# Mixer stage of a transformer block: convs, conv norm and conv half of the output product placed earlier, query-norm factors made in two halves

## The chip, the core and the metric

The kernel runs on one core of a Trainium2 chip. The metric is the device time of one execution in microseconds (us). The engines are PE (TensorE: matrix products, with PEld for the loads of its stationary operand), DVE (VectorE), ACT (ScalarE), POOL (GpSimd) and SP (SyncE, which issues the transfers). Each engine works through its own queue in the order in which the program was laid down and waits for others by semaphores.

## The reference, cut to what matters

The kernel computes two transformer layers' worth of blocks on a sequence of 512 positions with 1024 channels. The change lies in the first stage, the mixer (S = 512, 8 query heads of 64, 2 key heads; weights in fp32):

```python
def parallel_mixer(h, w_in, conv_dw, ..., w_out, tabs):
    z = jnp.einsum("bsd,dc->bsc", h, w_in)
    a_val, a_gate = z[..., :CONV_CH], z[..., CONV_CH:o0]
    q, k, v = ...
    a = a_val * jax.nn.sigmoid(a_gate)
    a = dwconv_centred(a, conv_dw, conv_dw_b)      # 31 taps, 512 channels
    a = layernorm(a, conv_ln_g, conv_ln_b)
    a = jax.nn.silu(a)
    q = apply_axial_rope(rmsnorm(q, q_norm_g), tabs)
    k = apply_axial_rope(rmsnorm(k, k_norm_g), tabs)
    att = gqa_blocked(q, k, v)
    mixed = jnp.concatenate([a, att], axis=-1)
    return jnp.einsum("bsc,cd->bsd", mixed, w_out)
```

Behind the mixer come a cross attention to a memory of 256 positions, five feed-forward stages, a pooling mixer and a latent attention. The keys and values of the memory do not depend on the mixer, and the kernel computes them inside it, as work that fills PE's waits.

## The kernel before

Activations lie as channels by positions, in tiles of 128 x 512. A product in fp32 precision is made of three passes (`mm3`, lines 182 to 184): weights and activations are each split into a rounded half `hi` and the rest `lo`. For weights `fetch` (L143) has SP load a tile of 128 x 1024 into one of three raw buffers; `cook` has ACT round it (`whi`, L152) and DVE subtract (`wlo`, L154), which frees the raw buffer.

The mixer, in the order of the program:

- *Projections.* `linear` over 14 column tiles of `w_in`, 24 products (8 x 3) each, in the order of `ORDER`: gate and value tiles in turn (`ev_gate`, `ev_val`, whose product `at` is a conv's input), the key tile, the value tile, four query tiles (`ev_q`). `ev_q` takes the sums of squares of the queries into one PSUM tile `qsum`; when all four are in, `inner_rstd` makes the factor `fcol` of all eight heads: a transpose on PE, then three Newton steps on DVE (L246 to L249).
- *Heads.* For each of 8 heads `scores` makes four score tiles (L707, L708), and `softmax_rows` their exponentials: maximum on DVE (L451), its product with the factor (`nb`, L452), exponential on ACT (L454), reciprocal on DVE (L455), scaling on POOL (L456). `attend` transposes the four results in blocks (L138 `pt`, four per block), ACT and DVE split each block (`pth`, `ptl`), and two products per block add up `po` (L723, L724). ACT copies half of it (`low`), DVE adds (`mixf`, L730). Two heads make one tile of `mix`. `scores(n + 1)` stands ahead of `attend(n)`.
- *Convs.* `conv` makes one of four 128-channel tiles: its weights take a raw buffer; 16 copies through SP (L587) bring the input at several shifts into the one set of tiles `cx`, so the copies of a conv wait for PE's end of the conv before. 24 products of 32 columns by 512 (L593, four of them side by side in PE), an evacuation by ACT, 7 taps by DVE (L602). They stand in the program at heads 0, 0, 1 and 2 (`CONV_AT`).
- *Conv norm.* `conv_norm` is a generator in three steps (mean, variance, the normalised and gated tiles `cv`), one step at each of heads 4, 5 and 6 (`CN_AT`).
- *Memory keys and values.* The generator `mem_kv` makes eight key tiles (24 products of 256 columns each) and 96 value products of 512 columns; two steps stand at each head (`KV_HEAD`).
- *Output product.* 8 column blocks in 8 PSUM tiles at once (all the PSUM there is), first the half of the attention (`mix`, 96 products), then that of the conv (`cv`, 96), then the evacuations.

What stands where in the queues is not the program's order alone: the tile framework lays the instructions down by their priority in the program and by when it thinks buffers and operands are there. So a step can stand ahead of others that the program names first, and buffers go to whoever the framework thinks can have them first.

```python
tags = ["ps", "ps", "po", "mi", "sc", "sc", "pt", "pt"]
pss = [self.ps(t, "wo") for t in tags]
for half, xh in ((0, mix), (1, cv)):
```

## Time and profile before

| | |
|---|---|
| median of 3 runs | 2541.47 us (2541.29 to 2543.51) |
| the profiled execution | 2543.81 us, its span 2542.0 us |
| busy: PE, DVE, ACT, POOL | 2491.3, 1305.2, 916.3, 301.8 us |
| granted clock of PE, mean | 0.996 |
| mixer, up to the warm-up products behind its output product | 302.69 us |

Times in the rows are from the span's start. A row of the view in order of time has the start, the duration, the engine, the line, the operation, output <- inputs, shapes and a count; in square brackets the time that the engine was idle before and what ended it. The ends of products are modelled, so that one can seem to overlap the next. Each key, value or weight tile has the name of its buffer (`raw`, `whi`, `wlo`); `ps` are products in PSUM, `sc` scores, `wo` the output product. The granted clock (PEclk) is a share of 2.4 GHz.

### The profile page before, as it was taken

The page shows a single profiled execution, that of the slowest core. Times are in us where ns is not written, and L with a number is a line of the kernel's source. Part 1 is how long each engine was busy: PE and PEld are TensorE (multiplying, and loading weights), DVE is VectorE, ACT ScalarE, POOL GpSimd, SP SyncE. Part 2 cuts the span into 40 slices and gives each one's busy share as a digit, 9 for nine tenths or more (in the row PEclk, how much of TensorE's full clock was granted, in tenths as well). Part 3 has the DMA queues.
Part 4 walks back from the last instruction along what each step waited for, and adds up shares of the span by engine and source line. Part 5 has one row for each costly group of instructions (what it writes and reads, how often), then busy time and mean ns, then how long its engine had stood idle before and what let it go on. Part 6 is the DMA issues. An engine that isn't in the chain of part 4 may idle for free.

```text
span 2542.0 us, 29816 instructions
## 1 busy us (share of the span) xinstructions
PE 2491.3 (98%) x11900; PEld 2015.1 (79%) x11900; DVE 1305.2 (51%) x1906; ACT 916.3 (36%) x1324; POOL 301.8 (12%) x285
## 2 busy tenths in 40 slices
PE   8898999999999999999999999999999999999999
PEld 6656677888887888888888888888887777888887
DVE  5777453766624554435555533554334685555522
ACT  4445444544423332224333222332223454423321
POOL 0011112111100111002111100111000012111100
PEclk9999999999999999999999999999999999999999
DMA  5143222232332223333223333232332211232332
GB/s 191 61 125 97 67 67 67 83 99 92 95 100 79 95 96 100 93 99 115 91 93 98 100 97 98 93 98 97 94 99 92 75 59 33 93 100 92 97 108 77
DMA packets 71851, 235.52 MB, mean 93 GB/s; under 512 B 8544, under 2 KB 12256, under 8 KB 71712
## 3 DMA queue, kind: packets, MB, share of 16 engines
q1 hardware_dynamic: 70336, 231.08, 29.1%
q0 software_dynamic: 1232, 2.36, 0.4%
q8 instruction: 93, 1.52, 0.2%
q14 instruction: 46, 0.38, 0.0%
q10 hardware_dynamic: 144, 0.18, 0.0%
HBM read 227.33 MB, written 2.10 MB: 90 GB/s over the span
## 4 chain that ended last, share of the span: by engine, by line
PE 94%; DVE 4%; ACT 1%; issue 1%; DMA 0%; ACTq 0%; DVEq 0%
PE ps L183 28%; PE ps L182 28%; PE ps L184 28%; PE cps L593 1%; PE pt L138 1%; PE sum L222 1%; PE bc L290 1%; PE wo L183 1%; PE wo L184 1%; PE wo L182 0%; PE po L724 0%; ACT whi L152 0%; DVE wlo L154 0%; PE po L183 0%; PE sc L182 0%
## 5 line engine op out<-in xcount | busy, mean ns | idle before, releaser
L152 ACT CAST whi<-raw 128x1024 fp32r<-128x1024 f32 (+2 forms) x432 | 440.2, 1021 | 1214.9 <-PE ps L183 754.1
L154 DVE TENSOR_TENSOR wlo<-raw,whi 128x1024 fp32r<-128x1024 f32 (+2 forms) x428 | 591.3, 1384 | 509.1 <-ACT whi L152 503.9
L182 PE MATMUL ps<-xh,whi 128*128 128x512 f32 x2008 | 782.7, 391 | 7.9 <-ACT xh L203 7.1
L183 PE MATMUL ps<-xl,whi 128*128 128x512 f32 x2008 | 785.5, 391 | 3.2 <-DVE xl L384 2.5
L184 PE MATMUL ps<-xh,wlo 128*128 128x512 f32 x2008 | 782.3, 390 | 0.0
L182 PEld LDWEIGHTS ps<-xh,whi 128*128 128x128 f32 x2008 | 377.7, 188 | 88.8 <-ACT xh L203 7.1
L183 PEld LDWEIGHTS ps<-xl,whi 128*128 128x128 f32 x2008 | 377.7, 188 | 87.3 <-DVE xl L384 6.1
L184 PEld LDWEIGHTS ps<-xh,wlo 128*128 128x128 f32 x2008 | 377.7, 188 | 78.1 <-issue 0.6
L182 PE MATMUL ps<-ah,whi 128*128 128x512 f32 x880 | 342.3, 389 | 0.0
L183 PE MATMUL ps<-al,whi 128*128 128x512 f32 x880 | 342.3, 389 | 0.0
L184 PE MATMUL ps<-ah,wlo 128*128 128x512 f32 x880 | 342.3, 389 | 0.0
L902 DVE TENSOR_TENSOR g<-ps,bct 128x512 f32<-128x512 f32 x176 | 120.7, 691 | 392.5 <-PE ps L184 384.2
L907 POOL TENSOR_TENSOR g<-g 128x512 f32<-128x512 f32 x88 | 118.9, 1351 | 887.3 <-ACT whi L152 624.4
L182 PEld LDWEIGHTS ps<-ah,whi 128*128 128x128 f32 x880 | 165.2, 188 | 34.3
L184 PEld LDWEIGHTS ps<-ah,wlo 128*128 128x128 f32 x880 | 165.2, 188 | 34.3
L183 PEld LDWEIGHTS ps<-al,whi 128*128 128x128 f32 x880 | 165.2, 188 | 34.2
L333 POOL TENSOR_TENSOR sq<-sq 128x512 f32<-128x512 f32 x54 | 81.5, 1510 | 582.0 <-ACT sq L326 581.4
L199 ACT CAST ah<-g 128x512 fp32r<-128x512 f32 x88 | 54.7, 622 | 113.3 <-POOL g L907 113.3
L456 POOL TENSOR_SCALAR p<-p,rl 128x512 f32<-128x512 f32 (+3 forms) x80 | 51.6, 650 | 334.5 <-DVE rl L455 277.0
L441 DVE SCALAR_TENSOR_TENSOR x<-ps,x 128x512 f32<-128x512 f32 x40 | 27.5, 691 | 84.5 <-PE ps L184 84.3
L201 DVE TENSOR_TENSOR al<-g,ah 128x512 fp32r<-128x512 f32 x88 | 63.1, 717 | 8.1 <-ACT ah L199 7.7
L454 ACT ACTIVATE p<-sc,nb,f 128x512 f32<-128x512 f32 (+3 forms) x80 | 53.5, 674 | 34.0 <-DVE nb L452 33.9
(293 smaller groups left out, 2314.5 us busy)
## 6 DMA issues: line engine op xcount, KB each, us to landing
raw<-in_wgu SPq DMA_DIRECT2D x176, 512.0 KB, 3.5
raw<-in_wd SPq DMA_DIRECT2D x64, 512.0 KB, 3.5
raw<-in_w_up SPq DMA_DIRECT2D x44, 512.0 KB, 3.5
raw<-in_wd SPq DMA_DIRECT2D x32, 384.0 KB, 3.1
raw<-in_w_down SPq DMA_DIRECT2D x16, 512.0 KB, 3.6
raw<-in_w_in SPq DMA_DIRECT2D x14, 512.0 KB, 3.7
raw<-in_mla_w_in SPq DMA_DIRECT2D x9, 512.0 KB, 3.5
raw<-in_mla_w_q SPq DMA_DIRECT2D x12, 384.0 KB, 3.0
```

The costliest lines, as they stand in the source:

```text
L152: self.nc.scalar.copy(hi[:, s], raw[:, s])
L154: eng.tensor_tensor(out=lo[:, s], in0=raw[:, s], in1=hi[:, s].bitcast(F32), op=ALU.subtract)
L182: mm(ps, w[0], x[0], start=start, stop=False)
L183: mm(ps, w[0], x[1], start=False, stop=False)
L184: self.mmi = mm(ps, w[1], x[0], start=False, stop=stop)
L199: nc.scalar.copy(hi, src)
L201: self.loi = eng.tensor_tensor(out=lo, in0=src, in1=hi.bitcast(F32), op=ALU.subtract)
L333: self.nc.gpsimd.tensor_tensor(out=sqs[0][:, :w], in0=sqs[0][:, :w], in1=sq[:, :w], op=ALU.add)
L454: nc.scalar.activation(p[:, :w], ps[:, :w], AF.Exp, bias=nb, scale=f, accum_out=l)
L456: nc.gpsimd.tensor_scalar(out=p[:, :w], in0=p[:, :w], scalar1=rl, scalar2=1.0, op0=ALU.mult, op1=ALU.mult)
L902: nc.vector.tensor_tensor(out=g, in0=ps, in1=rb, op=ALU.mult)
L907: nc.gpsimd.tensor_tensor(out=g, in0=g, in1=st["g"], op=ALU.mult)
```

## The change

Two convs go into the projections (behind the 7th and the 10th tile), two to head 0; the steps of the conv norm to heads 2, 3 and 4. The output product begins with the conv half: its column blocks 0 to 5 are made one by one in the `ps` tiles of PSUM and copied to SBUF by ACT (`part`), blocks 6 and 7 stay in PSUM; then comes the half of the attention, for blocks 0 to 5 into PSUM tiles that the heads have left, and DVE adds the parts. The factor of the query norms is made in two halves of four heads.

```diff
-    CONV_AT = (0, 0, 1, 2)
-    CN_AT = (4, 5, 6)
+    CONV_IN, CONV_AT = (6, 9), (0, 0)
+    CN_AT = (2, 3, 4)
...
-            i = nt - 10
+            i, o = (nt - 10) % 2, P * ((nt - 10) // 2)
             sq = self.square(ps)
-            self.sums([(self.c("blk64")[:, 32 * i:32 * i + 32], sq)], ps=qsum, start=i == 0,
-                      stop=i == 3)
+            self.sums([(self.c("blk64")[:, 32 * i:32 * i + 32], sq)], ps=qsum, o=o,
+                      start=i == 0, stop=i == 1)
+            if i == 1:
+                fcol.append(self.inner_rstd(qsum[:, o:o + P], 64, R1, 4, post=64.0 ** -0.5))
...
-        fcol = self.inner_rstd(qsum[:, :P], 64, R1, 8, post=64.0 ** -0.5)
+            if n in self.CONV_IN:
+                accs.append(self.conv(len(accs), ats[len(accs)]))
...
-                c = 8 * j + 2 * i + h
-                prs[n].append(self.softmax_rows(sc, S, fcol[:, c:c + 1], "xs"))
+                c = 4 * j + 2 * (i % 2) + h
+                prs[n].append(self.softmax_rows(sc, S, fcol[i // 2][:, c:c + 1], "xs"))
...
+        unit = lambda half, u: self.tiles(self.load_unit(a["w_out"][half, u]), 8)
+        parts = []
+        for u in range(4):
+            ws = unit(1, u)
...
+            for n2 in range(2):
+                ps = self.ps("ps", "wo")
+                for k in range(4):
+                    self.mm3(ps, ws[4 * n2 + k], cv[k], k == 0, u < 3 and k == 3)
+                if u < 3:
+                    nc.scalar.copy(room[n2], ps)
+                    parts.append(room[n2])
+                else:
+                    parts.append(ps)
         evac = self.post_collect("g_mixpost")
-        for nt in range(8):
-            evac(nt, pss[nt])
+        tags = ["sc", "sc", "po", "mi", "pt", "pt"]
+        for u in range(4):
+            ws = unit(0, u)
+            for n2 in range(2):
+                nt = 2 * u + n2
+                ps = parts[nt] if u == 3 else self.ps(tags[nt], "wo")
+                for k in range(4):
+                    self.mm3(ps, ws[4 * n2 + k], mix[k], u < 3 and k == 0, k == 3)
+                if u < 3:
+                    nc.vector.tensor_tensor(out=parts[nt], in0=ps, in1=parts[nt], op=ALU.add)
+                evac(nt, parts[nt])
```

Three places show how this moves instructions. The first is SP's queue where the loads of the memory's keys begin, before (`raw` with a number is one load into one of the three raw buffers, `in_conv_d` a conv's weights, `cx` a copy of a conv's input; in brackets the semaphores that the entry waits for):

```order
L143 DMA raw_1186<-in_conv_d 128x768 [waits DMAHW4_49,DMAHW2_49,DVE_49]
L487 DMA mem_769<-in_memT 128x2x256 [waits DMAHW7_49,DVE_49]
L143 DMA raw_1241<-in_w_mem_k 128x1024 [waits DMAHW5_49,DVE_49]
L143 DMA raw_1273<-in_w_mem_k 128x1024 [waits DMAHW4_49,DVE_49]
L143 DMA raw_1409<-in_conv_d 128x768 [waits DMAHW6_49,DMAHW5_49,DVE_49]
L587 DMA cx_254<-at_490 32x504 [waits PE_49]
```

and with the change:

```order
L588 DMA cx_257<-at_709 32x503 [waits DMAHW4_49]
L143 DMA raw_1315<-in_conv_d 128x768 [waits DMAHW5_49]
L143 DMA raw_1370<-in_w_mem_k 128x1024 [waits DMAHW6_49,DVE_49]
L143 DMA raw_1402<-in_w_mem_k 128x1024 [waits DMAHW7_49,DMAHW6_49,DVE_49]
L143 DMA raw_1543<-in_w_mem_k 128x1024 [waits DMAHW7_49,DMAHW0_49,DVE_49]
L143 DMA raw_1575<-in_w_mem_k 128x1024 [waits DMAHW1_49,DMAHW0_49,DVE_49]
L143 DMA raw_1713<-in_w_mem_k 128x1024 [waits DMAHW2_49,DMAHW1_49,DVE_49]
L143 DMA raw_1745<-in_w_mem_k 128x1024 [waits DMAHW3_49,DMAHW2_49,DVE_49]
L143 DMA raw_1895<-in_w_mem_k 128x1024 [waits DMAHW4_49,DMAHW3_49,DVE_49]
L143 DMA raw_1927<-in_w_mem_k 128x1024 [waits DMAHW5_49,DMAHW4_49,DVE_49]
L143 DMA raw_2112<-in_w_mem_v 128x1024 [waits DMAHW5_49,DVE_49]
L588 DMA cx_254<-at_910 32x504 [waits PE_49]
```

Before, two key tiles were loaded ahead of the second conv's copies and the others between later convs. Now all eight and the first value unit stand in a row, behind the 16 copies of the third conv, and each waits for the load before it and for DVE: they pass one raw buffer, while the other two hold the weights of the third and fourth conv.

The second place is DVE's queue at the factor of the query norms (`y_`, `b_`: Newton steps; `f_`: the factor; `nb_`: a score tile's maximum times it), before:

```order
L246 SCALAR_TENSOR_TENSOR b_967<-y_966,v_961 128x32
L248 TENSOR_TENSOR b_967<-b_967,y_966 128x32
L249 SCALAR_TENSOR_TENSOR y_966<-b_967,y_966 128x32
L277 SCALAR_TENSOR_TENSOR f_962<-y_966,y_238 128x32
L452 TENSOR_SCALAR nb_985<-mx_984,f_962 128x1
```

and with the change:

```order
L249 SCALAR_TENSOR_TENSOR y_960<-b_961,y_960 128x16
L533 TENSOR_TENSOR mk_1540<-ps_1549,mbc_115 128x256
L154 TENSOR_TENSOR wlo_1578<-raw_1575,whi_1577 128x1024
L246 SCALAR_TENSOR_TENSOR b_961<-y_960,v_955 128x16
L248 TENSOR_TENSOR b_961<-b_961,y_960 128x16
L249 SCALAR_TENSOR_TENSOR y_960<-b_961,y_960 128x16
L277 SCALAR_TENSOR_TENSOR f_956<-y_960,y_238 128x16
```

The `lo` half of the fourth key tile (`raw_1575` above) stands between the second and the last Newton step of the first half's factor now.

The third is PE's queue at the end of the last head (`po`; `mixh` is the half of the attention, `ch` that of the conv), before:

```order
L138 MATMUL pt_2480<-con_113,p_2317 128x128
L724 MATMUL po_2446<-ptl_2475,vh_589 128x512
L723 MATMUL po_2446<-pth_2485,vh_589 128x512
L724 MATMUL po_2446<-ptl_2486,vh_589 128x512
L182 MATMUL wo_2545<-mixh_1405,whi_2582 128x512
L183 MATMUL wo_2545<-mixl_1406,whi_2582 128x512
```

and with the change:

```order
L729 MATMUL po_2471<-pth_2499,vh_589 128x512
L182 MATMUL wo_2692<-ch_2180,whi_2675 128x512
L183 MATMUL wo_2692<-cl_2181,whi_2675 128x512
L184 MATMUL wo_2692<-ch_2180,wlo_2676 128x512
L730 MATMUL po_2471<-ptl_2500,vh_589 128x512
L729 MATMUL po_2471<-pth_2510,vh_589 128x512
L182 MATMUL wo_2729<-mixh_1534,whi_2707 128x512
L730 MATMUL po_2471<-ptl_2511,vh_589 128x512
```

Before, 147 products of the output stood behind the last product of the last head, and 92 of them and 4 more were the whole conv half. Now the conv half is through ahead of it, and 86 products of the other half are left. Behind the mixer only some neighbouring instructions change places, in later stages.

## Rows read from the trace of the kernel before

**Rows 1.** The page: the span.

```profile
span 2542.0 us, 29816 instructions
```

**Rows 2.** Two stretches of the mixer; columns as in the first line.

```profile
core 0: us, PE busy (x) PEld busy (x) DVE busy (x) ACT busy (x) POOL busy (x), PEclk, DMA share, GB/s
112.00:118.00 6.00, 5.44 (x16) 3.60 (x16) 3.87 (x11) 3.04 (x8) 2.78 (x4) 0.57 0.00 0
247.00:254.00 7.00, 3.58 (x11) 2.71 (x12) 3.93 (x8) 4.37 (x7) 0.00 (x0) 0.50 0.00 0
```

**Rows 3.** PE in order of time: start, duration, what; score products of head 0.

```profile
112.06 0.80 PE L707 MATMUL sc<-kh,st 128*128 128x512 f32 x1 [5.78 <-ACT p L454]
112.65 0.63 PE L708 MATMUL sc<-kl,st 128*128 128x512 f32 x1
113.08 0.63 PE L707 MATMUL sc<-kh,st 128*128 128x512 f32 x1
```

**Rows 4.** PE: a product of a key tile and the one 24 later.

```profile
103.01 0.28 PE L184 MATMUL ps<-mh,wlo 128*128 128x256 f32 x1
...
105.89 0.28 PE L184 MATMUL ps<-mh,wlo 128*128 128x256 f32 x1
```

**Rows 5.** PE: end of the tenth w_in tile.

```profile
74.12 0.39 PE L184 MATMUL ps<-xh,wlo 128*128 128x512 f32 x1
```

**Rows 6.** PE: 21 conv products in a row, two records each.

```profile
142.18 5.34 PE L593 MATMUL cps<-cx,raw 128*32 128x512 f32 x42
```

**Rows 7.** PE: four transposes of a head, and what starts after them.

```profile
148.02 0.60 PE L138 MATMUL pt<-con,p 128*128 128x128 f32 x4
148.38 0.36 PE L182 MATMUL ps<-mh,whi 128*128 128x256 f32 x1
```

**Rows 8.** SP: issues of two key tiles, and of the 16 copies of one conv tile.

```profile
82.69 6.35 SPq L143 DMA_DIRECT2D raw<-in_w_mem_k  x2
...
165.56 10.02 SPq L587 DMA_DIRECT2D cx<-at  x16
```

**Rows 9.** The DMA view: one of the copies, last number us to landing.

```profile
cx<-at SPq DMA_DIRECT2D x16, 64.0 KB, 2.0
```

**Rows 10.** ACT rounds two key tiles that share a raw buffer.

```profile
143.56 1.05 ACT L152 CAST whi<-raw 128x1024 fp32r<-128x1024 f32 x1
...
150.37 1.05 ACT L152 CAST whi<-raw 128x1024 fp32r<-128x1024 f32 x1 [4.63 <-DMA raw<-in_w_mem_k]
```

**Rows 11.** DVE ends heads 1, 5 and 7.

```profile
158.36 0.68 DVE L730 TENSOR_TENSOR mixf<-po,low 64x512 f32<-64x512 f32 x1
...
237.34 0.69 DVE L730 TENSOR_TENSOR mixf<-po,low 64x512 f32<-64x512 f32 x1 [2.98 <-ACT low L727]
...
268.49 0.68 DVE L730 TENSOR_TENSOR mixf<-po,low 64x512 f32<-64x512 f32 x1 [1.20 <-ACT low L727]
```

**Rows 12.** Groups by line and shape, 98 to 303 us: busy us, mean ns.

```profile
L154 DVE TENSOR_TENSOR wlo<-raw,whi 128x1024 fp32r<-128x1024 f32 x24 | 29.4, 1239 | 31.1 <-ACT whi L152 31.1
...
L454 ACT ACTIVATE p<-sc,nb,f 128x512 f32<-128x512 f32 x32 | 24.8, 777 | 24.8 <-DVE nb L452 24.8
L451 DVE TENSOR_REDUCE mx<-sc 128x1 f32<-128x512 f32 x32 | 21.7, 681 | 9.1 <-PE sc L708 9.0
L201 DVE TENSOR_TENSOR ptl<-pt,pth 128x512 fp32r<-128x512 f32 x32 | 21.6, 680 | 3.9 <-ACT pth L199 3.7
...
L199 ACT CAST pth<-pt 128x512 fp32r<-128x512 f32 x32 | 18.5, 586 | 8.5 <-PE pt L138 8.4
...
L452 DVE TENSOR_SCALAR nb<-mx,f 128x1 f32<-128x1 f32 x32 | 6.1, 204 | 0.2
...
L602 DVE SCALAR_TENSOR_TENSOR acc<-at,cwh,acc 128x504 f32<-128x504 f32 x8 | 5.9, 733 | 0.0
```

**Rows 13.** PE: after the last head, and the end of the product.

```profile
269.23 0.50 PE L182 MATMUL wo<-mixh,whi 128*128 128x512 f32 x1 [1.39 <-DVE mixf L730]
...
302.69 1.04 PE L435 MATMUL warm<-idb 128*128 128x512 bf16 x4
```

More of the change, by code (lines that the diff above doesn't have):

```diff
@@ L664, in ev_v @@
                 vh.append(hl)
-        qs = []
+        qs, fcol = [], []
         qsum = self.ps("po", "qsum")
         def ev_q(nt, ps):
-            i = nt - 10
+            i, o = (nt - 10) % 2, P * ((nt - 10) // 2)
             sq = self.square(ps)
-            self.sums([(self.c("blk64")[:, 32 * i:32 * i + 32], sq)], ps=qsum, start=i == 0,
-                      stop=i == 3)
+            self.sums([(self.c("blk64")[:, 32 * i:32 * i + 32], sq)], ps=qsum, o=o,
+                      start=i == 0, stop=i == 1)
+            if i == 1:
+                fcol.append(self.inner_rstd(qsum[:, o:o + P], 64, R1, 4, post=64.0 ** -0.5))
             qr = self.rope(ps, "gq", "gqs", cos, sin)
@@ L739, in mixer @@
             attend(n)
-            for i in range(4):
-                if n == self.CONV_AT[i]:
-                    accs.append(self.conv(i, ats[i]))
+            for _ in range(self.CONV_AT.count(n)):
+                accs.append(self.conv(len(accs), ats[len(accs)]))
             for _ in range(self.KV_HEAD):
@@ L747, in mixer @@
         self.wshare = self.W_OUT
-        tags = ["ps", "ps", "po", "mi", "sc", "sc", "pt", "pt"]
-        pss = [self.ps(t, "wo") for t in tags]
-        for half, xh in ((0, mix), (1, cv)):
-            for u in range(4):
-                ws = self.tiles(self.load_unit(a["w_out"][half, u]), 8)
-                for n2 in range(2):
-                    for k in range(4):
-                        self.mm3(pss[2 * u + n2], ws[4 * n2 + k], xh[k], half == 0 and k == 0,
-                                 half == 1 and k == 3)
-        evac = self.post_collect("g_mixpost")
-        for nt in range(8):
-            evac(nt, pss[nt])
+        unit = lambda half, u: self.tiles(self.load_unit(a["w_out"][half, u]), 8)
+        parts = []
+        for u in range(4):
+            ws = unit(1, u)
+            if u < 2:
+                room = self.big("part")
+                room = [room[:, :S], room[:, S:2 * S]]
+            elif u == 2:
+                room = [self.t("pr", name="part") for _ in range(2)]
+            for n2 in range(2):
[7 more added lines that the diff above has]
+                    parts.append(ps)
+        evac = self.post_collect("g_mixpost")
+        tags = ["sc", "sc", "po", "mi", "pt", "pt"]
[9 more added lines that the diff above has]
+                evac(nt, parts[nt])
     def conv_norm(self, accs, cv):
```

## The prediction

> **What bounds the kernel now.** I read the clock and busy table by stretches first, then PE in order of time in the mixer, then what ended its waits, then the queues of SP and DVE at those places. Behind the mixer PE works almost without a gap, and the change leaves the order of work there as it was, so only the first 303 us can move. The span is 2542.0 us [rows 1]; that execution took 2543.8 us as a whole, 2.3 above the median of 2541.47. I work out a difference on the span and take it off the median.
>
> In the mixer PE stands in two places. After the projections the first score products of head 0 are done, and the next one waits 5.78 us for an exponential, which waits for the factor of the query norms [rows 3]. Near the end PE holds the sums of the conv norm in its queue ahead of the last heads; there, from 247 to 254 us, it is busy 3.58 of 7 us at a granted clock of 0.50, and behind the first place at 0.57, that is near the lower of its two levels, 1.2 GHz [rows 2]. Heads 1 to 7 end at 158.36 to 268.49 us [rows 11]; PE takes up the out product at 269.23 and has done it by 302.69 [rows 13]. By the order, 147 products of 512 columns lie between, so one takes 0.228 us (33.46 / 147).
>
> **The change, part by part.** *Two convs move into the projections.* Their loads of weights there run tiles ahead of PE, so I price the move on PE alone: 21 conv products in a row take 5.34 us [rows 6], 24 take 6.1, two convs 12.2. That is work moved, not added. The tenth tile of w_in, which ends at 74.4 (74.12 and one product) [rows 5], and the second conv behind it end at 86.6.
>
> *SP's queue.* The 16 copies of the third conv wait for that second conv and take SP 10.0 us. All eight key tiles of the memory stand behind them, so the first is issued at 96.6 instead of 82.69 [rows 8]. Two of the three raw buffers now hold conv weights until those convs have run. Key tiles go through the third, one after the other. One such turn (rounding by ACT, the lo half by DVE, the next load) takes 6.81 us from one rounding to the next [rows 10]. I take this for each, so the seventh key tile is ready 7 x 6.81 = 47.7 us later, at 144.3.
>
> *Query factors in two halves.* These add one transpose and some 15 DVE instructions of about 0.2 us, as the small ones that scale a maximum [rows 12], 3 us. What they should hide, the 5.78 us, is hidden by key products now. But DVE has the lo half of the fourth key tile ahead of the last Newton steps, so the early factor comes no earlier than that tile. I cost the halves at nothing: the key chain covers them. Without that cover they would cost their 3 us.
>
> *The chain through the third and fourth conv.* PE's queue has seven key tiles ahead of the third conv: the seventh takes 2.88 [rows 4], the conv 6.1, to 153.3. The fourth conv's copies take 10.0 and 2.0 to land [rows 8, 9], to 165.3; its last 21 products stand behind the last of them, 5.3, to 170.6. ACT's evacuation is nearest to a 0.59 us cast [rows 12], to 171.2. Then DVE has, up to the end of head 1, 7 taps, 4 maxima, 7 small ones, 2 lo halves of 512 columns, 4 of 1024 and the head's own sum: 5.1 + 2.7 + 1.4 + 1.4 + 5.0 + 0.7 = 16.3 [rows 12]. Head 1 ends at 187.5, 28 us later than before, but with all the convs, all the keys and half the values done.
>
> *Heads 2 to 7.* For each I add up what the three queues hold between the ends of two heads, with the durations of [rows 12] and 0.228 per product and 0.09 per transpose [rows 7]; the largest of the three is the head's least time. Head 2 on DVE: 4 maxima, 5 splits, 7 small, 1 sum, 8.1. In this way DVE sets heads 2 to 4 with 8.1, 16.6 and 18.8, ACT head 5 with 11.1, PE heads 6 and 7 with 13.4 and 14.0 (46 and 48 out products among them): 82.0. The same count for heads 2 to 5 of the kernel before gives 18.2 + 22.6 + 15.1 + 19.8 = 75.7, and they took 79.0 (158.36 to 237.34), 1.043 times as much. So 82.0 x 1.043 = 85.5, and the last head ends at 273.0, 4.5 us later than before. The six copies and six adds of the partial products are in these counts or beside the last products, 3.5 and 4.1 us in all.
>
> *The end.* 0.74 us later (as from 268.49 to 269.23) PE goes on. All 96 products of the conv half are ahead of the last head now, so 86 remain: 19.6 us, to 293.3. Before it was 302.69. The work of the evacuation behind the last product is the same, since the last two column blocks stay in PSUM. **Sum: 9.4 us less**, 2541.5 - 9.4 = 2532.
>
> On the clock, the rows show a fall behind a wait of 5.78 us [rows 2, 3]. In the key chain PE will have some 3 us of wait in each turn (6.8 less 2.9 and about 1 of head work), shorter than that one; my sum takes the upper level there. The Trainium skill (TensorE: Matmul & The Clock Gate, the section HAM oscillation — how this bites in real kernels) says that short bursts of products between waits for loads can start at the lower clock again each time. By that rule the sum would be that of the second rival; the trace agrees for the 5.78 us wait and leaves shorter ones open.
>
> **The rivals.** *All overlaps* (chance 0.17). For it: two issues of key tiles together once took 6.35 us, and an issue is up to 0.63 of that (10.02 / 16 for a copy) [rows 8], so one turn was 5.7 to 6.35, in the middle 6.0, and nothing forces the factor 1.043. Then 7 x 0.8 = 5.6 and 3.5 more are saved: 18.5 less, 2523.
> *The lower clock in the key chain* (0.18). A 512-column product takes 0.43 us there [rows 3] for 0.228. The seventh key tile and the third conv, on the chain, double: 9.0 later, 2541, no change. For it: the waits in each turn; against it: the head's work between.
> *The key chain is slower than its load* (0.15). A lo half that waits on DVE behind work that itself waits for PE lengthens every turn, as the one for the sixth key tile does, behind two maxima of head 1. The gain is gone at a turn of 8.2 us (6.8 + 9.4 / 7). At 9.5, a turn and four such instructions, it is 18.8 later: 9.4 slower, 2551. For it: in 31.1 us DVE waited for a rounding before a lo half [rows 12]. Against it: before, the maxima were between them as well, and the turn was 6.81.
> That the change does not do what it says can only hold for the early factor, above, and is in the sum.
>
> **How the numbers follow.** My own case has 0.50, 2526 to 2538 by a turn 0.8 us shorter or longer. About 5 us (0.2%) is what a measurement of this kernel tells from no change. Of my case nearly all lies below 2536.4, the first rival lies there whole: faster 0.65. The second, and the upper edge of mine: same 0.20. The third: slower 0.15. The range leaves out the third and a little of the first: 2519 to 2546.
>
> **What would show it.** Right: PE's wait of 5.78 us is gone, replaced by several of about 3 us that end on lo halves of key tiles; roundings of key tiles 6 to 7 us apart; head 1 ends near 187, head 7 near 273, the warm-up products begin near 293; no stretch at 0.50 near the conv norm. Wrong: turns above 8 us; waits of PE for loads of w_in in the projections, which I cost at nothing (their loads lead by two tiles, and a stall there would come on top whole); a last head that ends after 283.

## The result: slower by 0.5%, and the profile after

The changed kernel takes 2554.59 us (median of 5 runs, 2553.44 to 2556.74) where the kernel before takes 2543.51 beside it: a ratio on record of 1.0051, with a 95% interval of 1.0040 to 1.0063 (these two medians alone give 1.0044; in the larger batches beside the experiments the kernel before has medians of 2541.91 to 2542.78). The forecast was 2532.0, with a range of 2519 to 2546. One execution of one experiment below took 8835.65 us; it is left out (the other one of that run took 2543.32), and the run was repeated.

The profiled execution has this span (from the page; before: [rows 1]):

```profile
span 2552.8 us, 29839 instructions
```

It is 10.8 us longer. Three places make it up, each found by the same event in both traces:

| | before | after | difference |
|---|---|---|---|
| end of the output product (first warm-up products) | 302.69 | 307.66 | 5.0 |
| from there to the first operands of the next stage | 28.61 | 30.72 | 2.1 |
| latent attention, from its first scores to its output product | 76.44 | 79.87 | 3.4 |

The rest between these points differs by 0.3 us in all. The two traces do not start level: 16 broadcast products of the projections, ahead of any conv, stand 1.65 us earlier in the changed kernel, so that counted from there the mixer loses 6.6 us and not 5.0. Before and after, PE in order of time:

```profile
52.03 1.58 PE L290 MATMUL bc<-con,f 128*64 128x128 f32 x16
...
50.38 1.58 PE L290 MATMUL bc<-con,f 128*64 128x128 f32 x16
```

The mixer, step by step, as the prediction had it:

| | predicted | before | after |
|---|---|---|---|
| second early conv ends | 86.6 | - | 86.25 |
| first key tile of the memory is issued | 96.6 | 82.69 | 96.18 |
| turn of a key tile through the one buffer | 6.81 | - | 6.28 |
| fourth conv ends | 170.6 | 183.69 | 169.13 |
| head 1 ends | 187.5 | 158.36 | 183.93 |
| heads 2 to 4 | 45.4 | 58.0 | 62.5 |
| heads 5 to 7 | 40.2 | 52.1 | 43.1 |
| head 7 ends | 273.0 | 268.49 | 289.57 |
| products behind it | 86 | 147 | 79 |
| output product ends | 293.3 | 302.69 | 307.66 |

The ends of the heads, DVE in order of time (start, duration, engine, line, operation; before: [rows 11]):

```profile
183.93 0.68 DVE L736 TENSOR_TENSOR mixf<-po,low 64x512 f32<-64x512 f32 x1
192.62 0.68 DVE L736 TENSOR_TENSOR mixf<-po,low 64x512 f32<-64x512 f32 x1 [0.42 <-ACT low L733]
213.31 0.68 DVE L736 TENSOR_TENSOR mixf<-po,low 64x512 f32<-64x512 f32 x1
246.47 0.67 DVE L736 TENSOR_TENSOR mixf<-po,low 64x512 f32<-64x512 f32 x1
...
289.57 0.68 DVE L736 TENSOR_TENSOR mixf<-po,low 64x512 f32<-64x512 f32 x1
```

Up to head 1 (the first row) all went about as forecast, 3.6 us early. Then head 4 takes 33.2 us, from 213.31 to 246.47. PE is not busy there, as the stretches show (columns as in [rows 2]):

```profile
core 0: us, PE busy (x) PEld busy (x) DVE busy (x) ACT busy (x) POOL busy (x), PEclk, DMA share, GB/s
112.00:118.00 6.00, 6.00 (x56) 5.67 (x55) 5.01 (x14) 2.68 (x4) 0.00 (x0) 1.00 0.28 86
120.00:140.00 20.00, 15.71 (x106) 13.36 (x106) 15.33 (x48) 10.29 (x20) 4.12 (x6) 1.00 0.24 79
193.00:216.00 23.00, 14.59 (x44) 9.20 (x44) 16.37 (x41) 13.11 (x30) 9.16 (x11) 0.78 0.01 1
...
230.00:257.00 27.00, 15.84 (x58) 12.11 (x57) 18.80 (x41) 17.79 (x33) 3.06 (x4) 0.69 0.18 59
```

The wait at 106 us and the lower clock behind it are gone: PE is busy in all of 112 to 118, at full clock, where it had 0.57 [rows 2]. In their place stand two thin stretches, 193 to 216 and 230 to 257, with 8.4 and 11.2 us without a product and a mean clock of 0.78 and 0.69. The conv norm is in both. What held head 4 can be read off its rows, here those of PE, ACT and DVE in order of time:

```profile
210.86 0.60 PE L138 MATMUL pt<-con,p 128*128 128x128 f32 x4
...
212.97 2.19 ACT L326 ACTIVATE sq<-acc 128x512 f32<-128x512 f32 x4
...
216.71 0.79 PE L182 MATMUL ps<-whi,mh 128*128 128x512 f32 x1 [3.46 <-DVE mvl L204]
...
222.44 0.65 PE L222 MATMUL sum<-sq,con 128*32 128x128 f32 x16
...
224.72 1.05 ACT L152 CAST whi<-raw 128x1024 fp32r<-128x1024 f32 x1 [7.76 <-PE ps L184]
...
227.28 0.27 PE L138 MATMUL tr<-con,q 128*128 128x128 f32 x1
...
230.76 1.04 ACT L152 CAST whi<-raw 128x1024 fp32r<-128x1024 f32 x1 [2.23 <-DMA raw<-in_w_out]
...
233.67 2.04 PE L290 MATMUL bc<-con,y 128*128 128x128 f32 x8 [3.36 <-DVE y L249]
...
235.75 0.59 ACT L297 COPY bct<-bc 128x512 f32<-128x512 f32 x1 [3.95 <-PE bc L290]
236.23 1.08 ACT L199 CAST pth<-pt 128x512 fp32r<-128x512 f32 x2
...
236.88 0.80 PE L729 MATMUL po<-pth,vh 128*128 128x512 f32 x1 [1.16 <-ACT pth L199]
```

The last transposes of the first two blocks of head 4 (first row) are done by 211.5. Their casts on ACT run at 236.23, some 25 us later, and PE's next product of a head at 236.88. The casts wait for nothing of their own: they stand in ACT's queue behind four roundings of output weights, of which the first waits 7.76 us for value products on PE and the last 2.23 us for its load, and behind `bct`, the copy of the norm's factor, which waits 3.95 us for the norm's chain. In that chain the squares are through at 215.2; their sums stand in PE's queue behind value products that themselves began late, at 216.71; the transpose of the sums stands behind more of them; the Newton steps stand on DVE between the `lo` halves of the output weights; the broadcast waits 3.36 us for the last of them.

### The profile page after: what moved, and what is told of

It is laid out like the page before. It is cut to its first block, busy times and chain, and to the rows that moved or that the text cites. A ratio compares the mean times of both kernels' runs of the same rounds, so it can differ in the third digit from the quotient of the medians.

```text
span 2552.8 us, 29839 instructions
## 1 busy us (share of the span) xinstructions
PE 2494.4 (98%) x11901; PEld 2018.6 (79%) x11901; DVE 1315.9 (52%) x1928; ACT 921.2 (36%) x1330; POOL 304.3 (12%) x285
## 4 chain that ended last, share of the span: by engine, by line
PE 94%; DVE 4%; ACT 1%; issue 1%; DMA 0%; POOL 0%; ACTq 0%; POOLq 0%
PE ps L182 28%; PE ps L183 28%; PE ps L184 28%; PE cps L594 1%; PE pt L138 1%; PE sum L222 1%; PE bc L290 1%; DVE wlo L154 1%; PE wo L182 1%; ACT whi L152 1%; PE wo L183 1%; PE wo L184 0%; PE po L730 0%; PE po L182 0%; PE po L183 0%
## 5 line engine op out<-in xcount | busy, mean ns | idle before, releaser
L184 PEld LDWEIGHTS ps<-xh,wlo 128*128 128x128 f32 x2008 | 377.4, 188 | 78.7 <-issue 0.8
L454 ACT ACTIVATE p<-sc,nb,f 128x512 f32<-128x512 f32 (+3 forms) x80 | 53.6, 676 | 33.3 <-DVE nb L452 31.9
```

What stands on the lines that cost most here:

```text
L184: self.mmi = mm(ps, w[1], x[0], start=False, stop=stop)
L454: nc.scalar.activation(p[:, :w], ps[:, :w], AF.Exp, bias=nb, scale=f, accum_out=l)
```

## The experiments

Each is given as the edit to the changed kernel unless it says otherwise. The time of a head runs from the end of the head before it to its own end.

The time of a run moves behind the mixer too. Read from the traces as in the first table, against the changed kernel (us; the start of a trace varies by up to 1.8):

| run | output product ends | to the next stage | latent attention | span |
|---|---|---|---|---|
| values early | -2.2 | +2.0 | -3.3 | -3.5 |
| norm late | -1.3 | -2.1 | -2.5 | -5.9 |
| output product as before | +2.1 | -2.1 | -3.4 | -3.5 |
| convs as before | +1.2 | -0.6 | -4.1 | -3.7 |
| norm: link cut | -1.3 | 0.0 | -3.4 | -4.6 |
| norm: without broadcast | -8.8 | -0.6 | -4.9 | -14.2 |
| norm: without factor | -15.8 | -0.5 | -4.9 | -21.1 |
| norm at head 2 | -4.6 | -0.5 | -4.9 | -9.8 |
| one pass, as changed | -18.7 | -0.5 | -1.2 | -20.4 |
| one pass, norm at head 2 | -11.9 | -0.5 | -4.9 | -17.2 |
| one pass, values early | -12.2 | +2.6 | -1.2 | -10.8 |

So a part of the mixer is priced by the end of the output product, and not by the time alone.

### Four parts undone, one at a time

**Values early.** Theory A: the first pair of value sums, done at 181 us, is evacuated only at 215 to 217, so that 48 value products cannot fill waits. Theory B: the norm stands too early.

```diff
-    KV_HEAD = 2
+    KV_HEADS = (4, 4, 4, 4, 0, 0, 0, 0)
```

> The changed kernel with one difference: the sixteen steps of the memory's keys and values stand at heads 0 to 3, four each, in place of two at each of eight heads, so that the first value pair's evacuation stands in ACT's queue right behind head 1. Theory A (stuck values: in the changed kernel the first pair of value sums is complete at 181 us, but its evacuation stands behind the norm's squares in ACT's queue and runs at 215 to 217, so that 48 value products, 10.9 us of PE, cannot cover the waits of heads 2 and 3): the evacuation now runs before 190, the 48 products fall into the waits of heads 2 and 3, head 4 ends 8 to 11 us earlier than 246.5, the time is about 2544. Theory B (the norm is too early: its sums, squares and scalings stand ahead of the heads' maxima and splits on DVE and ACT, whatever PE has): the products move, but heads 2 to 4 end within 3 us of where they do now, the time is 2552 to 2557.

2551.13 us. The evacuation moved to 185.22 and all value products were done by 204.98, as A wanted. But head 4 ended at 244.83, 1.6 us earlier; heads 2 to 4 took 57.4 us in place of 62.5, with heads 2 and 4 at 17.7 and 21.4 (8.7 and 33.2). Heads 3 and 4 gained 2.4 and 11.8 us, and head 2 lost 9.0 of them. The time lies between the two forecasts. A explains some 5 us of heads 2 to 4 and 2.2 of the output product's end; the 2.2 are lost again by the next stage, and what is left of the 3.5 us is the latent attention's.

**Norm late.**

```diff
-    CN_AT = (2, 3, 4)
+    CN_AT = (4, 5, 6)
```

> The changed kernel with the steps of the conv norm back at heads 4, 5 and 6. Theory A (stuck values): heads 2 and 3 lose the norm's work, and the evacuation of the values stands ahead of the norm; but the norm's chain then stands at heads 5 and 6 with no value products beside it and the conv half of the output product starts later, so the time stays within 4 us of 2554.6. Theory B (norm too early): heads 2 to 4 get back the 12 us or so that the norm's instructions take on DVE there (8.6 us of sums and scalings and the waits they make), head 4 ends before 236, and the time is 2542 to 2546.

2548.71 us, between the two forecasts. In the heads it is B, as the rows of DVE in order of time show:

```profile
186.25 0.68 DVE L736 TENSOR_TENSOR mixf<-po,low 64x512 f32<-64x512 f32 x1
194.96 0.68 DVE L736 TENSOR_TENSOR mixf<-po,low 64x512 f32<-64x512 f32 x1 [0.42 <-ACT low L733]
204.52 0.68 DVE L736 TENSOR_TENSOR mixf<-po,low 64x512 f32<-64x512 f32 x1 [0.41 <-ACT low L733]
212.13 0.68 DVE L736 TENSOR_TENSOR mixf<-po,low 64x512 f32<-64x512 f32 x1 [0.54 <-ACT low L733]
...
270.18 0.69 DVE L736 TENSOR_TENSOR mixf<-po,low 64x512 f32<-64x512 f32 x1
```

Without the norm in them heads 2 to 4 take 25.9 us in place of 62.5, and the last head ends 19.4 us earlier. But the conv half, which goes first, could begin only at 258.51, when the norm was done; all 192 products stood behind that, 159 of them behind the last head, and the output product ended at 306.40, 1.3 us earlier; the rest of the 5.9 us lies behind it. The output product that begins with the conv half turns a late norm into a late product.

**Output product as before.** The function's last part is that of the kernel before.

> The changed kernel with the output product as it was before (eight column blocks in all of PSUM, the half of the attention first). Both theories: heads 2 to 4 are unchanged, since the order of ACT is the same up to the end of head 4, so head 4 ends within 1 us of 246.5. Behind it PE has only the products of the finished mix tiles to fill waits with, and some 147 products of 0.228 us are left behind the last head in place of 86: 13.9 us more, less some 2 us for the shorter evacuation: 2564 to 2568. If the new output product is itself a loss, the time is below 2554.

2552.54 us: below the forecast of 2564 to 2568, and 2 us below the changed kernel. Head 4 ended at 246.60, as expected. Without the conv half among them heads 5 to 7 took 27.4 us in place of 43.1; the 147 products left then ended the product at 309.76, 2.1 us later. The new output product brings 2.1 us at its end and gives them back on the way to the next stage (below); the 2 us of the time are in the latent attention, 3.4 us shorter here.

**Convs as before.**

```diff
-    CONV_IN, CONV_AT = (6, 9), (0, 0)
+    CONV_IN, CONV_AT = (), (0, 0, 1, 2)
```

> The changed kernel with the four convs back at heads 0, 0, 1 and 2. Theory C (the early convs use up the cover: the key and value products are all done by 181 us, where they lasted to 223 before): the key products spread again over heads 1 to 3, and the time is below that of before, 2536 to 2541. Theories A and B: the first value pair's evacuation still stands behind the norm's mean, and the norm, at heads 2 to 4, now waits for the fourth conv as well; the time is 2550 to 2562.

2550.17 us: theory C falls. Key products lasted to 193, and heads 0 to 2 ended within 4.2 us of where they did before, but head 3 took 43.9 us and head 4 26.4, and the output product ended at 308.89. Wherever the key products stand, the heads with the early norm are long.

### Parts alone

**Convs and halves, norm and output product as before.** `CN_AT = (4, 5, 6)`, and the output product of before.

> The kernel before with the two convs in the projections and the two factors of four heads; the conv norm (heads 4, 5, 6) and the output product stay as before. Theory D (the norm is a serial chain over DVE, ACT and PE, and the heads that it is laid into wait with it): heads 2 to 4 stay as short as in the run with the norm late, 25 to 30 us together, so three mix tiles are ready by 236; up to 72 of their products, 16.4 us, can fill the waits of heads 5 to 7, which the output product that begins with the conv half could not give; the output product ends at 290 to 297 where it was 302.7, the time is 2531 to 2537. Theory E (the load of DVE and ACT sets the heads, wherever its pieces stand): the last head ends at 268 to 272 as before, some 147 products stand behind it, the time is 2541 to 2544.

2542.05 us beside 2542.68: ratio 0.9998 (0.9988 to 1.0007), no change. Heads 2 to 4 took 25.2 us, as theory D said, but the gain went: heads 5 and 6, which hold the norm now, took 23.5 and 21.9, the last head ended at 265.78 (268.49 before), and 147 products stood behind it as before. The forecast of 72 products as cover failed: 45 of the 192 ran ahead of the last head's end, as before. By the code a column block needs a PSUM tile, and six of the eight belong to the heads; that this is the limit was not tried.

**Convs alone.** The same without the two factors.

> The kernel before with the two convs in the projections alone (one factor of eight heads, conv norm and output product as before). If the halves of the factor are worth nothing, as the prediction costs them, the time is within 2 us of that of the convs with the halves. If the early factor lets scores begin ahead of the key tiles, the first exponential comes 3 to 6 us later without it, and the time is that much longer.

2541.93 us, ratio 0.9997 (0.9988 to 1.0007): the halves of the factor are worth nothing here, as the prediction costed them.

### What holds the heads with the norm

**The norm without its factor.**

```diff
-            sqs = self.gather(sqs, self.square(accs[i]), i == 3)
-        rc = self.bcast(self.rstd(sqs, 512))
+        rc = self.con[:, :S]
```

> The changed kernel without the squares, sums, transposes, Newton steps and the broadcast of the conv norm: the scaling multiplies by a constant tile in their place, so the norm's factor is left out. Removed on DVE 2.1 us, on ACT 2.8, on PE some 3. Theory D: head 4 ends by more than these, at 236 or before (it was 246.5), since the chain of 22.8 us from the first square (213.0) to the broadcast (235.75) is gone; the conv half starts 8 us or more earlier than 256.7; the time is 2542 to 2548. Theory E: head 4 ends 2 to 3 us earlier, the time is 2551 to 2553.

2534.23 us, 20.4 less, more than theory D asked for. In the mixer it is 15.8: head 4 took 13.4 us in place of 33.2 for some 3 us less work on each engine, and the output product ended at 291.91. DVE ends heads 3 and 4:

```profile
214.50 0.68 DVE L736 TENSOR_TENSOR mixf<-po,low 64x512 f32<-64x512 f32 x1
227.92 0.68 DVE L736 TENSOR_TENSOR mixf<-po,low 64x512 f32<-64x512 f32 x1
```

**Its data link cut.**

```diff
-        rc = self.bcast(self.rstd(sqs, 512))
+        self.bcast(self.rstd(sqs, 512))
+        rc = self.con[:, :S]
```

> The changed kernel with every instruction of the conv norm, but the scaling multiplies by a constant tile in place of the broadcast factor, which is made and not used. The load is the whole of before. Theory D, if the chain binds through the scaling on DVE: as in the run without the factor, within 3 us. Theory D, if it binds through PE's queue, where the broadcast's products wait for the Newton steps with the heads' products behind them: head 4 gains less than half of what it gains there. Theory E: nothing changes, 2553 to 2556.

2549.96 us, head 4 30.2: 3 us less. So the scaling that needs the factor does not hold the head; having the instructions that make the factor in the queues does. The rows of ACT in order of time say how: the casts of head 4 stand behind the roundings of output weights and the copy `bct` here as well, though nothing reads it:

```profile
229.04 1.05 ACT L152 CAST whi<-raw 128x1024 fp32r<-128x1024 f32 x1 [7.24 <-PE ps L184]
...
235.04 1.04 ACT L152 CAST whi<-raw 128x1024 fp32r<-128x1024 f32 x1 [2.21 <-DMA raw<-in_w_out]
235.99 0.58 ACT L297 COPY bct<-bc 128x512 f32<-128x512 f32 x1
236.46 1.08 ACT L199 CAST pth<-pt 128x512 fp32r<-128x512 f32 x2
```

Here ACT waited 7.24 us for PE and 2.21 for a load, both ahead of a rounding, and for the broadcast not at all: `bct` runs right behind the last rounding.

**Without the broadcast.** Squares, sums, transpose and Newton steps stay; the eight products and the copy go. Run twice.

```diff
-        rc = self.bcast(self.rstd(sqs, 512))
+        self.rstd(sqs, 512)
+        rc = self.con[:, :S]
```

> The changed kernel with the squares, sums, transpose and Newton steps of the conv norm kept, and only its last link left out: the eight broadcast products on PE and their copy on ACT; the scaling multiplies by a constant tile. Removed on PE some 1.1 us, on ACT 0.6. Cutting the data link alone gave head 4 30.2 us (33.2 with the chain, 13.4 without sums, Newton steps and broadcast). If what holds head 4 is that the broadcast stands in PE's and ACT's queues ahead of the head's own products and casts while it waits for the Newton steps (queue theory): head 4 ends at 232 or before, time 2534 to 2542. If it is what stands ahead of the broadcast (the sums, which have the value products ahead of them, and the Newton steps among the roundings of the output weights): head 4 stays at 27 us or more, time 2547 to 2552.

> The same edit as the run without the broadcast, whose one undisturbed execution took 2543.3 us. Queue theory (the broadcast waits in the queues of PE and ACT ahead of the head's own work): head 4 at 22 us or less where it was 33.2, time 2541 to 2546. If what stands ahead of the broadcast holds it: head 4 at 27 us or more.

2541.28 us: 8.7 us less than with the unused broadcast, 7.5 of them at the end of the output product, for 1.7 us of work (1.13 on PE, 0.59 on ACT). Head 4 took 23.7 us, between the two forecasts. ACT in order of time has the first of the two casts where it can run, right behind the squares, and the roundings of output weights only behind it:

```profile
212.57 2.19 ACT L326 ACTIVATE sq<-acc 128x512 f32<-128x512 f32 x4
214.78 0.58 ACT L199 CAST pth<-pt 128x512 fp32r<-128x512 f32 x1
...
230.55 1.05 ACT L152 CAST whi<-raw 128x1024 fp32r<-128x1024 f32 x1 [0.52 <-PE ps L184]
```

So the unused broadcast costs little by its own wait. With it the framework lays head 4's casts behind the roundings, which wait for PE and a load; without it, ahead of them. That this place alone makes the 7.5 us was not tried.

At the end of the output product the 15.8 us that the factor costs fall apart into 1.3 for the scaling that needs it (307.66 to 306.35), 7.5 for the broadcast and its copy (to 298.84) and 6.9 for the squares, sums and Newton steps (to 291.91). The rest of the 20.4 us lies behind the mixer, most of it in the latent attention. Each edit moves other instructions too, so the split is rough.

**All steps of the norm at head 2.** `CN_AT = (2, 2, 2)`, taken by count.

> The changed kernel with all three steps of the conv norm at head 2, instead of one each at heads 2, 3 and 4. Chain theory: the links then follow each other without a head's maxima and splits between them, so one head is long in place of three; the tiles of the conv half are there by 225 in place of 255, the output product covers heads 4 to 7, heads 2 to 4 together take 45 us or less (62.5), time 2540 to 2547. Load theory: the same work in the same span, heads 2 to 4 together 58 to 65 us, time 2551 to 2557.

2547.35 us. The tiles of the conv half were there at 226, but heads 2 to 4 took 62.7 us (8.4, 42.4 and 11.8): head 3 now waited as heads 3 and 4 had. On the heads the load theory's number came out, on the time neither: the gain of 7 us is in the product, which began 4.3 us earlier, and in the stages behind. Putting the links closer together did shorten the chain, to 23.1 us from the first addition `tot` to the copy `bct` (193.39 to 216.48) from 42.5 (193.23 to 235.75), but not the heads.

### A shorter chain

The variance as the mean square less the squared mean needs no mean product ahead of the squares (cut to the lines that matter):

```diff
-        nc.tensor.matmul(mp, self.c("ones")[:, 0:1].to_broadcast([P, P]), tot, start=True,
...
+        sm = self.sums([(self.c("ones"), x) for x in accs], ps=ps)
+        sqs = [self.square(x) for x in accs]
+        s2 = self.sums([(self.c("ones"), sq) for sq in sqs], ps=ps, o=P)
...
+        R = self.newton(mm, 4)
...
         yield
...
-            nc.vector.tensor_tensor(out=accs[i], in0=accs[i], in1=mean, op=ALU.subtract)
-            sqs = self.gather(sqs, self.square(accs[i]), i == 3)
-        rc = self.bcast(self.rstd(sqs, 512))
+        rc = self.bcast(R)
+        mrc = self.bcast(nm)
         yield
```

A `yield` ends a step of the norm. So the edit does two things: it takes links out of the chain, and it moves the squares, sums and Newton steps from the second step into the first, which leaves the broadcasts a step of their own. Only where all steps stand at one head is it the shorter chain alone.

It was run in four places. (In the last record below, 57.1 and 63.8 are the sums of heads 3 to 5; those of heads 2 to 4 are 55.3 and 62.7.)

> The kernel before with the two early convs, the two factors, and a conv norm of one pass: the variance is the mean square less the squared mean, from sums that PE takes of the conv tiles and of their squares at once; mean and factor are broadcast together. It takes the mean product, its copy, the subtraction and the wait between them out of the chain (some 8 us), adds 32 small products and a few small DVE steps. Chain theory: heads 5 and 6 (23.5 and 21.9 us with the two-pass norm) lose 6 to 9 us together, the time is 2533 to 2537 (2542.05). Load theory: 2540 to 2543.

> The changed kernel with the one-pass norm, all its steps at head 2. Chain theory: 4 to 8 us less than the run with the two-pass norm at once, by the links that are gone. Load theory: within 2 us of it.

> The kernel before with the one-pass norm and nothing else. If the gain of the one-pass norm needs no part of the change: 2535 to 2538, as with the early convs (2536.5). If the early convs are needed for it: 2539 to 2543.

> The changed kernel, steps of the norm at heads 2, 3 and 4, with the one-pass norm. If the number of links sets the price: heads 2 to 4 together 51 to 56 us (62.5; 57.1 with the one-pass norm at once against 63.8 with two passes at once), time 2542 to 2548. If the queue order at head 4 sets it, the one-pass norm gains under 3 us here: 2551 to 2555.

| place of the norm | two passes | one pass | product ends, one pass |
|---|---|---|---|
| kernel before | 2541.9 | 2538.15 | 295.79 |
| early convs, halves, norm late | 2542.05 | 2536.45 | 293.88 |
| the change, norm at head 2 | 2547.35 | 2538.16 | 295.81 |
| the change as it is | 2554.59 | 2535.36 | 288.95 |

The largest gain, 19 us (18.7 of it at the end of the output product), is where the change put the norm; the expectation there was 2542 to 2548. But there the squares also start a head earlier, at 193.07 in place of 212.97, and the last `bct` at 216.50 in place of 235.75; how much of the gain is this earlier place was not tried. The kernel is now faster than both: 0.9974 (0.9965 to 0.9983) of before. DVE and PE in order of time:

```profile
184.38 0.68 DVE L736 TENSOR_TENSOR mixf<-po,low 64x512 f32<-64x512 f32 x1
...
229.05 0.67 DVE L736 TENSOR_TENSOR mixf<-po,low 64x512 f32<-64x512 f32 x1
...
270.86 0.68 DVE L736 TENSOR_TENSOR mixf<-po,low 64x512 f32<-64x512 f32 x1
...
288.95 1.04 PE L435 MATMUL warm<-idb 128*128 128x512 bf16 x4
```

Heads 2 to 4 take 44.7 us, heads 5 to 7 41.8. The shorter norm gains 3.8 us in the kernel before (0.9988, 0.9978 to 0.9997), so it needs no part of the change; with the change it is 2.8 us better still, though the two intervals overlap a little. Norm at head 2 and one pass, the run that shortens the chain alone: 9.2 us better than two passes, 7.3 of them at the end of the output product, where the chain theory asked for 4 to 8. The last `bct` starts 7.8 us earlier. ACT in order of time, with two passes and with one:

```profile
216.48 0.59 ACT L297 COPY bct<-bc 128x512 f32<-128x512 f32 x1 [4.60 <-PE bc L290]
...
208.71 0.59 ACT L297 COPY bct<-bc 128x512 f32<-128x512 f32 x1 [2.88 <-PE bc L290]
```

**One pass, values early.** The norm at head 2, and the key and value steps at heads 0 to 3.

> The changed kernel with the one-pass norm at head 2 and the key and value steps at heads 0 to 3, so that the value products and their evacuation stand ahead of the sums and both PSUM tiles are free when the conv half could begin. If the value products ahead of the sums still cost: the conv half begins before 235 (245.1), time 2528 to 2534. If not: within 3 us of 2538.2.

2546.26 us, a miss: the conv half did begin early, at 223.29, but head 3 took 36.6 and head 4 15.2 us, with no value products left beside the chain, and the next stage began 33.3 us behind the product. The product ended at 295.47, 0.3 us earlier than with the norm at head 2 and the values as they were: its early start is worth nothing where the heads pay for it. The 8.1 us that this run is slower lie behind it: 3.1 on the way to the next stage and 3.7 in the latent attention (6.4 us of span in all).

### Behind the output product

With the change POOL adds up the squares of the output's column blocks after the last products. After, PE and POOL in order of time:

```profile
303.05 7.27 POOL L333 TENSOR_TENSOR sq<-sq 128x512 f32<-128x512 f32 x4 [0.56 <-ACT sq L326]
...
307.66 1.04 PE L435 MATMUL warm<-idb 128*128 128x512 bf16 x4
310.37 0.65 PE L222 MATMUL sum<-sq,con 128*32 128x128 f32 x16 [1.68 <-POOL sq L333]
```

ACT's squares of all six blocks stood behind a rounding of output weights that waited 6.06 us for PE, so they and POOL's additions came in a row at the end. The same wait for POOL is 3.95 and 4.41 us in the two runs with the values early, and in the run with the norm late, with the same output product, there is none and the next stage comes after 28.63 us. With the one-pass norm, the six additions on DVE:

```diff
-            st["sqs"] = self.gather(st["sqs"], sq, nt == ND - 1)
+            if gname == "g_mixpost" and 0 < nt < ND - 1:
+                s0 = st["sqs"][0]
+                self.nc.vector.tensor_tensor(out=s0, in0=s0, in1=sq, op=ALU.add)
```

> The one-pass norm with the placing of the change, and the six additions of the output product's squares on DVE in place of POOL. If POOL's additions hold the end of the mixer: the 1.67 us wait of the sums for POOL is gone, the next stage's wait for its first operands ends 28.6 us behind the product as in the kernel before (30.2 now), time 2533 to 2535. If not: the time is within 1 us of 2535.4 and the wait has another name.

2534.57 us, ratio 0.9972 (0.9961 to 0.9983). The wait for POOL is gone; the first operands of the next stage come 28.87 us behind the product (30.21 without the edit, 28.61 before):

```profile
292.46 0.42 PE L222 MATMUL sum<-sq,con 128*32 128x128 f32 x8 [0.38 <-ACT sq L326]
```

The time itself moved by less than two medians can tell apart.

## Why the prediction was wrong, point by point

- **Two convs in the projections, SP's queue, the one buffer: right,** the times in part by luck. The second conv ended at 86.25 (86.6), the first key tile was issued at 96.18 (96.6), in a trace that runs 1.65 us ahead of the one forecast from; from a common start both came 1.2 to 1.3 us late. And ACT's roundings of the first and the seventh key tile stand six turns of 6.28 us apart (6.81 by [rows 10]):

```profile
100.59 1.05 ACT L152 CAST whi<-raw 128x1024 fp32r<-128x1024 f32 x1 [2.20 <-DMA raw<-in_w_mem_k]
...
138.24 1.05 ACT L152 CAST whi<-raw 128x1024 fp32r<-128x1024 f32 x1 [1.78 <-DMA raw<-in_w_mem_k]
```

- **Head 1 and the fourth conv: right,** 183.93 for 187.5 and 169.13 for 170.6, early by the shorter turns and the early start.
- **The clock in the key chain: right that it stays up.** PE's waits there were 0.27 to 1.51 us, not the some 3 forecast, and the granted clock was 1.00 from 120 to 140 us. The rule cited there from the Trainium skill (TensorE: Matmul & The Clock Gate, HAM oscillation — how this bites in real kernels), by which bursts between waits for loads start at the lower clock, is told there of longer waits than these. The trace agrees with it in heads 3 and 4: behind waits of 3.77 and 3.46 us, at 203.70 and 216.71, products of 512 columns followed at 0.43 us, the lower level, where they come at 0.23 at the upper. But short waits close together did it too: behind 0.83, 0.49 and 0.76 us, between 182 and 186, the granted clock from 186.18 to 188.70 was 0.50 (columns as in [rows 2]):

```profile
186.18:188.70 2.52, 2.52 (x9) 1.98 (x8) 1.98 (x7) 1.02 (x3) 1.65 (x2) 0.50 0.08 33
```

  So the lower-clock rival came true in the wrong place.
- **Heads 2 to 7: wrong, and this is the step that failed.** I took the largest of three queue sums for each head, times 1.043: 85.5 us; they took 105.6. Of the 20.1 us too few, 17.1 are in heads 2 to 4 (62.5 for 45.4), and 13.6 of those in head 4. The largest of three sums holds only while the queues feed each other without long waits. The factor 1.043 came from heads 2 to 5 of the kernel before, which hold of the norm only the mean and its subtraction; the norm's own stretch there, 247 to 254 us, stood in [rows 2] as a loss, and I moved its instructions without its waits. The runs put a price on it: the factor of the norm costs head 4 19.8 us for some 3 us of work, and 7.5 us of the output product's end go with a broadcast and its copy, 1.7 us of work, since with them head 4's casts stand behind roundings that wait. With the norm out of them the three heads took 25.9 us, with the one-pass norm 44.7. With head 1 3.6 us early and the end 2.2 shorter, the 20.1 us make the output product 14.4 late (307.66 for 293.3). The sign named for it, a last head that ends after 283, came: 289.57.
- **Heads 5 to 7: nearly right,** 43.1 for 40.2.
- **The end: right in kind.** 79 products behind the last head for 86, 18.1 us for 20.3. That the conv half is through by then holds; against the run with the old output product it was worth 2.1 us and no more, since the 96 products stretch heads 5 to 7 by 15.7. Before, all 96 of the conv half are among the 147 in the trace, none of them ahead of the last head.
- **"The work of the evacuation behind the last product is the same": wrong by 2.1 us,** POOL's additions.
- **That the order of work behind the mixer stays as it was: wrong by 3.4 us,** in the latent attention, which no edit touches (last section).
- **The factor in two halves: right at nothing.**
- **The rivals.** The third had the right sign and nearly the time (2551), by another cause, so by luck: the turn was 6.28 us, never 8.2. The price of a wait that takes the place of the one removed was not on the list for the conv norm, though both thin stretches of [rows 2] were read.

## What to carry to other kernels

When a serial chain over several engines (sums, a transpose, small steps, a broadcast, a copy) is moved among other work, price not its instructions but the order that the queues get by it: what the heads' own work then stands behind in each engine's queue, and what that waits for. Eight small products and a copy that nobody reads moved two casts behind four roundings, and the output product ended 7.5 us later with them. The largest of the queues' sums is a lower bound for such a stretch, and the place to look for the surplus is the same chain's stretch in the profile of before. No place tried for the two-pass norm beat the kernel before (2541.93 to 2554.59 us); with one pass five of the six runs did (2534.57 to 2538.16). Price a stage at its own end, since a stage far behind can move by as much as the change.

## What the runs showed of the hardware and the layout that was not expected

- **A stage that no edit touches moved by up to 4.9 us.** From the first scores of the latent attention to its output product the runs took from 75.0 us (the norm without its factor) to 79.9 (the change): the changed kernel and that with the old output product reach it within 0.02 us of each other and leave it 3.44 apart. Of the changed kernel:

```profile
2070.85 0.39 PE L182 MATMUL sc<-knh,qnh 128*128 128x256 f32 x1 [0.84 <-ACT knh L199]
...
2150.72 0.74 PE L182 MATMUL ps<-oh,whi 128*128 128x512 f32 x2 [0.35 <-ACT oh L199]
```

  With the old output product:

```profile
2070.83 0.38 PE L182 MATMUL sc<-knh,qnh 128*128 128x256 f32 x1 [0.84 <-ACT knh L199]
...
2147.28 0.96 PE L182 MATMUL ps<-oh,whi 128*128 128x512 f32 x3 [0.48 <-ACT oh L199]
```

  The instructions are the same, some neighbours in the queues of PE, DVE and ACT are not. Over this stage the order of the three queues (by operation, names and shapes, buffer numbers left out) is one and the same in ten of the 18 traces read, the kernel before and the old output product among them: 75.0 to 76.6 us. The order of the changed kernel stands in four more, all with the one-pass norm: 78.7 to 79.9. Three runs have other orders, 76.5 to 77.4. So the layout of a far stage depends on what comes before it, and the changed kernel's order goes with the 3.4 us, a third of this change's loss, and about as much as a measurement can tell; which of the swaps costs what was not tried. Up to 1.6 us come within one order, from a cause that stays open.
- **A broadcast whose result nobody reads cost 8.7 us,** 7.5 of them in the mixer, for 1.7 us of work: 2549.96 with it, 2541.28 without. Its own waits were nearly nothing; the order of ACT's queue changed with it.
- The time between the start of the span and the first conv differs by up to 1.5 us between the runs with early convs (53.78 to 55.28), so single times of two traces compare to about that.
